# Score products of two attention maps: full-height products first, half-height rests side by side, mask added on VectorE

## The chip, the core and the metric

The kernel runs on one core of a Trainium2 chip. The metric is the device time of one execution in microseconds. The names used below: PE is TensorE's matmul, PEld its weight load, DVE is VectorE, ACT is ScalarE, POOL is GpSimd, SP is the engine that issues most DMAs.

## What is computed

A decoder block on 1024 tokens of width 1024. Two mixers run in parallel, a differential attention of 4 heads and a short gated convolution. They are merged by sigmoid gates, projected and normalised, and a routed mixture of 32 experts (two per token) follows. The change lies in the attention alone, cut here to its core:

```python
s = jnp.einsum('bhmqd,bhmkd->bhmqk', qi, kt) * scale     # m: two maps, head width 64
mask = kpos[None, :] <= qpos[:, None]
p = jax.nn.softmax(jnp.where(mask, s, neg), axis=-1)
a = p[:, :, 0] - lam * p[:, :, 1]
return jnp.einsum('bhqk,bhkv->bhqv', a, vt)              # in blocks of 128 queries
```

## The kernel before, in words

The program runs in stages. First come the projections of q, k and v (`first_part`, products `psq` of 256 columns, lines 372 to 374) and the convolution branch (`pc`). Then comes the attention, from about 306 us to 603 us of the trace. Merging projections (`projections`), the mixing product with routing (`mixing`), and the experts with the last normalisation follow.

The attention loops over 4 heads and, in each, over 8 blocks of 128 queries; block i has (i + 1) * 128 keys (`kw`). Heads 0 to 2 take the blocks in rising order, head 3 in falling order. For each block `scores` makes two score maps, and `values` turns the pair of the block before into the head's output. Between the two stand the gate products (`gates`, tile `psg`, lines 389 to 391): 24 products of 512 columns per call, two calls per block for the first 4 blocks and one for each later block, until after 28 blocks all 32 calls are used up. The last 4 blocks of head 3 (512 keys and fewer) have none.

Every factor of a score is split into a high and a low part, so that q k = qh kh + ql kh + qh kl. The head width is 64, half of TensorE's 128 rows, and `prep` uses that: `kh` holds the high part of k twice, on both halves of the rows, and `qh` holds the high part of q on one half and the low part on the other. So one product over all 128 rows (line 478) gives qh kh + ql kh, the combined product. The rest, qh kl, is a product over 64 rows (line 481): rows 0 to 63 for map 0 and rows 64 to 127 for map 1, since that is where `qh` and `kl` of the map lie. Scores are made in pieces of up to 512 columns, at least 256 wide.

Before the rest of a map's last piece, line 480 multiplies an identity by the mask tile (`identb`, `maskb`, 128 columns, bf16) and accumulates that on the block's diagonal. Then VectorE takes the row maxima (line 483), ScalarE the exponentials with their sums (line 485), and `values` scales them (lines 493 to 496), transposes the result on TensorE (line 503, `tp`), copies it out of PSUM on VectorE (line 504, `ct`) and multiplies by v (line 507, `po`). The score tiles come from the pool `psc` with 2 buffers of 1024 columns.

A scheduler orders the instructions of each engine when the program is built; the chip runs each engine's list in order. The core of a map's products:

```python
T.matmul(ps[:, c:c + n], q, kh[:, c:c + n], start=True, stop=False)
if c + 512 >= kw:
    T.matmul(ps[:, i * P:kw], K.identb, K.maskb, start=False, stop=False, skip_group_check=True)
T.matmul(ps[:, c:c + n], q[a], kl[:, c:c + n], start=False, stop=True)
```

Of the kernel before, what the change touches and what calls it, by code (L numbers as in the profile page):

```python
# [11 lines left out]
F32 = mybir.dt.float32  # L12
F32R = mybir.dt.float32r
BF16 = mybir.dt.bfloat16
# [8 lines left out]
P = 128  # L23
S = 1024
# [151 lines left out]
def constants(K):  # L176
    nc, tc = K.nc, K.tc
    G, V = nc.gpsimd, nc.vector
    const = K.const
    K.ident = const.tile([P, P], F32, name="ident")  # L180
    make_identity(nc, K.ident)

    K.cols = const.tile([P, 48], F32, name="cols")

    K.lam = const.tile([P, 2], F32, name="lam")
    K.epss = const.tile([P, 1], F32, name="epss")
    K.epsc = const.tile([P, 1], F32, name="epsc")
    G.memset(K.epsc, EPS)
    K.one1 = const.tile([P, 1], F32, name="one1")
    K.maskb = const.tile([P, P], BF16, name="maskb")  # L190
    K.identb = const.tile([P, P], BF16, name="identb")
    V.tensor_copy(K.identb, K.ident)
    K.ssq = const.tile([P, HEADS, NT], F32, name="ssq")

    K.L = const.tile([P, NT, 40], F32, name="L")
    K.gm = const.tile([P, NT, 8], F32, name="gm")
    K.em = const.tile([P, NT, 8], F32, name="em")

    K.aw = const.tile([P, NT, 2], F32, name="aw")

    K.second = const.tile([P, N_COLS], F32, name="second")
    K.gidx = const.tile([P, N_COLS], I32, name="gidx")
    K.sidx = const.tile([P, N_COLS], I32, name="sidx")

    K.rows = const.tile([P, 256], F32, name="rows")

    K.order = const.tile([P, 32], I32, name="order")
    K.over = const.tile([P, 32], I32, name="over")
    K.omax = const.tile([P, 1], I32, name="omax")
    dram = K.dram  # L210

    K.h_dram = dram.tile([S, DW], F32, name="h_dram")

    K.y_dram = dram.tile([2 * S, D], F32, name="y_dram")
    K.y_views = dram_disjoint_views(K.y_dram, N_COLS)
    K.g_dram = dram.tile([P, 16, S], F32, name="g_dram")
    K.z_dram = dram.tile([P, 4, 2, S], F32, name="z_dram")
# [71 lines left out]
def first_part(K, stL, stR):  # L289
# [3 lines left out]
    V, A, G, T, SY = nc.vector, nc.scalar, nc.gpsimd, nc.tensor, nc.sync  # L293
# [29 lines left out]
    with ExitStack() as st:  # L323
# [38 lines left out]
        for c in range(6):  # L362
# [3 lines left out]
            for tb in range(NT):  # L366
                if c == 0 and tb >= 2:
                    load_x(tb)
                ps = psb.tile([P, 512], F32, name="psq")[:, 0:256]
# [25 lines left out]
    with ExitStack() as st:  # L395
        cv = st.enter_context(tc.tile_pool(name="cv", bufs=2, side="right", reuse_waits="tile"))
        pc = st.enter_context(tc.tile_pool(name="pc", bufs=5, space=PSUM, reuse_waits="tile"))
        n = 0
# [40 lines left out]
    sc = ExitStack()  # L439
    psc = sc.enter_context(tc.tile_pool(name="psc", bufs=2, space=PSUM, reuse_waits="tile"))  # L440
# [6 lines left out]
    def prep(h):  # L447

        kh = [kq.tile([P, S], F32R, name=f"kh{m}") for m in range(2)]
        kl = kq.tile([P, S], F32R, name="kl")  # L450
        qh = [kq.tile([P, S], F32R, name=f"qh{m}") for m in range(2)]
        for src, is_k in ((ks, True), (qs, False)):
            for g in range(2):
                gs = slice(g * 512, g * 512 + 512)
                ps = ps1.tile([P, 512], F32, name="tp")
                for b in range(4):
                    T.transpose(ps[:, b * P:(b + 1) * P], src[g][:, b, h * P:(h + 1) * P], ident)
                for m, (a, b) in enumerate(((LO, HI), (HI, LO))):
                    if is_k:
                        A.copy(kh[m][a, gs], ps[a])  # L460
                        V.tensor_sub(kl[a, gs], ps[a], kh[m][a, gs].bitcast(F32))
                        G.tensor_copy(kh[m][b, gs], kh[m][a, gs].bitcast(F32))
                    else:
                        A.copy(qh[m][a, gs], ps[a])
                        V.tensor_sub(qh[m][b, gs], ps[a], qh[m][a, gs].bitcast(F32))
        return [(kh[m], kl[a], qh[m], a) for m, a in enumerate((LO, HI))]

    def scores(maps, i):
        kw = (i + 1) * P
        res = []  # L470
        s = sm.tile([P, 2], F32, name="s")
        for m in range(2):
            kh, kl, qh, a = maps[m]
            ps = psc.tile([P, S], F32, name="sc")
            for c in range(0, kw, 512):
                n = max(256, min(512, kw - c))
                q = qh[:, i * P:(i + 1) * P]
                T.matmul(ps[:, c:c + n], q, kh[:, c:c + n], start=True, stop=False)
                if c + 512 >= kw:
                    T.matmul(ps[:, i * P:kw], K.identb, K.maskb, start=False, stop=False, skip_group_check=True)  # L480
                T.matmul(ps[:, c:c + n], q[a], kl[:, c:c + n], start=False, stop=True)  # L481
            nm = sm.tile([P, 1], F32, name="nm")
            V.tensor_reduce(nm, ps[:, 0:kw], axis=AX.X, op=ALU.max, negate=True)  # L483
            p = pp.tile([P, S], F32, name=f"p{m}")
            A.activation(p[:, 0:kw], ps[:, 0:kw], AF.Exp, bias=nm, scale=1.0, accum_out=s[:, m:m + 1])  # L485
            res.append(p)
        return res, s
# [50 lines left out]
    n = 0  # L538
    maps = prep(0)
    for h in range(HEADS):  # L540
        for i in order(h):
            cur = scores(maps, i)
            for _ in range(2 if n < 8 else 1):
                if n < 32:
                    gates(n)
                    n += 1
                    if n == 32:
                        sx.close()
                        open_proj(K, stL, w1, piece)
            if pend is not None:  # L550
                values(*pend)
            pend = (h, i, *cur)
            if i == 3 and h + 1 < HEADS:
                nxt = prep(h + 1)
        if h + 1 < HEADS:
            maps = nxt
# [920 lines left out]
@with_exitstack  # L1477
def block_kernel(ctx: ExitStack, tc: tile.TileContext, x, positions, w_in, b_gate, lq1, lk1, lq2, lk2, subln_g,
                 w_o_att, conv_w, w_o_conv, w_mix, ln1_g, ln1_b, w_rg, b_rg, w_re, b_re, w_eg, w_eu, w_ed,
                 ln2_g, ln2_b, out):  # L1480
    K = Ctx()
    for name, ap in list(locals().items()):
        if name not in ("ctx", "K"):
            setattr(K, name, ap)
    K.nc = tc.nc
    K.const = ctx.enter_context(tc.tile_pool(name="const", bufs=1, side="left"))
    K.dram = ctx.enter_context(tc.tile_pool(name="dram", bufs=1, space=DRAM))
    constants(K)
    K.stM = ctx.enter_context(ExitStack())
    K.stP = ExitStack()  # L1490
    stL, stR = ExitStack(), ExitStack()
    first_part(K, stL, stR)
    projections(K, stR)
    K.stP.close()
    mixing(K, stL, stR)
    stR.close()
    experts(K)
    combine(K)
    K.stM.close()
# [22 lines left out]
```

## Time and profile before

| | |
|---|---|
| device time, median of 3 runs | 1428.47 us (1427.58 to 1430.57) |
| the profiled execution | 1428.7 us, of which the span of its instructions is 1426.7 us |
| PE busy | 1308.1 us, 92% of the span |
| DVE busy | 697.0 us, 49% |
| ACT busy | 487.5 us, 34% |
| DMA | 301.75 MB, mean 211 GB/s |
| mean granted TensorE clock | 0.966 |

The busy time of PE counts each matmul from its start to the end of its results, and matmuls overlap like that: what one costs is read from the distance between the starts of neighbours. In the timeline rows the first number is the start in us and the second the duration; an "xN" at the end merges N equal neighbours.

### The profile page before, as it was taken

To read this page: it belongs to the slowest core of one execution; us is meant where nothing else is said; L and a number is where in the kernel's file an instruction comes from. 1 tells how busy PE (TensorE), PEld (TensorE's weight loads), DVE (VectorE), ACT (ScalarE), POOL (GpSimd) and SP (SyncE) were. 2 spreads that over 40 slices of the span, in tenths; PEclk is the share of its full clock that TensorE was granted. 3 is DMA by queue.
4 is the path that set the end of the run, shared out by engine and by line. 5 is a ranking of instruction groups with operands and counts; after the bars stand their busy time and mean duration, and the time that the engine had idled before them with its cause. 6 is when DMAs were issued, how large, how long until landed. Compare 5 with 4: busy or idle time off the path is not lost. (4 is left out here: it accounts for less than half of the span.)

```text
span 1426.7 us, 17850 instructions
## 1 busy us (share of the span) xinstructions
PE 1308.1 (92%) x6771; PEld 938.4 (66%) x6771; DVE 697.0 (49%) x1254; ACT 487.5 (34%) x837; POOL 137.3 (10%) x213
## 2 busy tenths in 40 slices
PE   7999999999999999999999948999999998999830
PEld 7999888877777777778788735654555544454310
DVE  6431133243535355476566656654554544453338
ACT  4102111144545455442221235532343333342125
POOL 1330000000000001000000120000110011000005
PEclk9999999999999999999999969999999999999975
DMA  7112121122121310364654277699999999999946
GB/s 241 52 39 60 45 74 60 59 74 75 46 73 53 104 59 16 140 224 148 216 206 148 104 227 275 241 414 421 420 420 402 409 419 419 420 409 406 420 182 242
DMA packets 101240, 301.75 MB, mean 211 GB/s; under 512 B 13550, under 2 KB 56603, under 8 KB 76571
## 3 DMA queue, kind: packets, MB, share of 16 engines
q1 hardware_dynamic: 93370, 279.54, 51.4%
q0 software_dynamic: 7776, 21.00, 3.8%
q8 instruction: 55, 0.90, 0.3%
q14 instruction: 39, 0.31, 0.1%
HBM read 274.81 MB, written 33.04 MB: 216 GB/s over the span
## 5 line engine op out<-in xcount | busy, mean ns | idle before, releaser
L173 DVE TENSOR_TENSOR wlo<-m,whi 128x1024 fp32r<-128x1024 f32 x72 | 87.1, 1223 | 70.6 <-ACT whi L172 68.3
L372 PE MATMUL psq<-wh,xh 128*128 128x256 f32 x384 | 109.3, 285 | 0.7 <-ACT xh L172 0.7
L373 PE MATMUL psq<-wl,xh 128*128 128x256 f32 x384 | 108.2, 282 | 0.0
L374 PE MATMUL psq<-wh,xl 128*128 128x256 f32 x384 | 107.7, 281 | 0.0
L172 ACT CAST wh<-wr 128x1024 fp32r<-128x1024 f32 x41 | 43.0, 1052 | 187.3 <-PE pc L390 64.9
L389 PE MATMUL psg<-xh,wh 128*128 128x512 f32 x256 | 104.9, 410 | 0.0
L391 PE MATMUL psg<-xh,wl 128*128 128x512 f32 x256 | 102.2, 399 | 0.0
L390 PE MATMUL psg<-xl,wh 128*128 128x512 f32 x256 | 102.1, 399 | 0.0
L172 ACT CAST whi<-m 128x1024 fp32r<-128x1024 f32 x72 | 74.6, 1050 | 58.1 <-PE g L1075 20.4
L173 DVE TENSOR_TENSOR wl<-wr,wh 128x1024 fp32r<-128x1024 f32 x41 | 51.8, 1266 | 82.8 <-ACT wh L172 82.6
L761 PE MATMUL pm<-wmh,m 128*128 128x512 f32 x256 | 77.1, 406 | 0.0
L390 PE MATMUL pc<-xl,wh 128*128 128x512 f32 x192 | 75.9, 396 | 0.0
L389 PE MATMUL pc<-xh,wh 128*128 128x512 f32 x192 | 75.9, 396 | 0.0
L391 PE MATMUL pc<-xh,wl 128*128 128x512 f32 x192 | 75.9, 395 | 0.0
L372 PEld LDWEIGHTS psq<-wh,xh 128*128 128x128 f32 x384 | 72.9, 190 | 1.5 <-ACT xh L172 1.4
L373 PEld LDWEIGHTS psq<-wl,xh 128*128 128x128 f32 x384 | 73.1, 190 | 0.0
L374 PEld LDWEIGHTS psq<-wh,xl 128*128 128x128 f32 x384 | 72.9, 190 | 0.2 <-DVE xl L173 0.2
L485 ACT ACTIVATE p<-sc,nm 128x128 f32<-128x128 f32 (+7 forms) x64 | 47.4, 741 | 48.3 <-DVE nm L483 20.5
L504 DVE COPY ct<-tp 128x512 f32<-128x512 f32 (+3 forms) x48 | 26.7, 557 | 72.6 <-PE tp L503 72.3
L483 DVE TENSOR_REDUCE nm<-sc 128x1 f32<-128x128 f32 (+7 forms) x64 | 48.4, 756 | 28.2 <-PE sc L481 28.0
L389 PEld LDWEIGHTS psg<-xh,wh 128*128 128x128 f32 x256 | 48.1, 188 | 13.9 <-issue 2.6
L391 PEld LDWEIGHTS psg<-xh,wl 128*128 128x128 f32 x256 | 48.1, 188 | 10.7
(429 smaller groups left out, 2924.5 us busy)
## 6 DMA issues: line engine op xcount, KB each, us to landing
m<-in_w_exp_down_dram SPq DMA_DIRECT2D x32, 1024.0 KB, 20.1
m<-in_w_exp_up_dram SPq DMA_DIRECT2D x32, 1024.0 KB, 20.6
m<-in_w_exp_gate_dram SPq DMA_DIRECT2D x24, 1024.0 KB, 19.8
wr<-in_w_in_dram SPq DMA_DIRECT2D x40, 512.0 KB, 4.3
raw<-in_w_exp_down_dram SPq DMA_DIRECT2D x20, 1024.0 KB, 20.8
raw<-in_w_exp_up_dram SPq DMA_DIRECT2D x13, 1024.0 KB, 13.1
raw<-in_w_exp_gate_dram SPq DMA_DIRECT2D x12, 1024.0 KB, 20.1
rawY<-in_w_exp_gate_dram SPq DMA_DIRECT2D x12, 1024.0 KB, 21.1
```

What stands on the lines that cost most here:

```text
L172: nc.scalar.copy(hi, raw)
L173: nc.vector.tensor_sub(lo, raw, hi.bitcast(F32))
L372: T.matmul(ps, xh[:, k, ts], wh[k], start=k == 0, stop=False)
L373: T.matmul(ps, xh[:, k, ts], wl[k], start=False, stop=False)
L374: T.matmul(ps, xl[:, k, ts], wh[k], start=False, stop=k == KD - 1)
L389: T.matmul(ps, hi[:, k], xh[:, k, hs], start=k == 0, stop=False)
L390: T.matmul(ps, hi[:, k], xl[:, k, hs], start=False, stop=False)
L391: T.matmul(ps, lo[:, k], xh[:, k, hs], start=False, stop=k == KD - 1)
L483: V.tensor_reduce(nm, ps[:, 0:kw], axis=AX.X, op=ALU.max, negate=True)
L485: A.activation(p[:, 0:kw], ps[:, 0:kw], AF.Exp, bias=nm, scale=1.0, accum_out=s[:, m:m + 1])
L504: V.tensor_copy(ct[:, g * P:(g + nb) * P], ps[:, 0:nb * P])
L761: T.matmul(ps[:, hs], a[:, k], w[:, hs], start=k == 0 and i == 0, stop=k == KD - 1 and i == 2)
```

## The change

`scores` now takes both maps' tiles at once. It issues the combined products of map 0 and of map 1 for all pieces, and then the rests piece by piece, map 0 and map 1 in turn, so that a product on the upper half of the rows stands beside one on the lower half. The identity product is gone, and with it `identb` and its cast. In its place VectorE adds `maskb` to the diagonal 128 columns of each score tile in PSUM, ahead of the row maxima. Nothing else is edited.

```diff
--- before.py
+++ after.py
@@ -188,8 +188,6 @@
     G.memset(K.epsc, EPS)
     K.one1 = const.tile([P, 1], F32, name="one1")
     K.maskb = const.tile([P, P], BF16, name="maskb")
-    K.identb = const.tile([P, P], BF16, name="identb")
-    V.tensor_copy(K.identb, K.ident)
     K.ssq = const.tile([P, HEADS, NT], F32, name="ssq")
 
     K.L = const.tile([P, NT, 40], F32, name="L")
@@ -469,16 +467,18 @@
         kw = (i + 1) * P
         res = []
         s = sm.tile([P, 2], F32, name="s")
+        pss = [psc.tile([P, S], F32, name="sc") for _ in range(2)]
+        parts = [(c, max(256, min(512, kw - c))) for c in range(0, kw, 512)]
+        for ps, (kh, kl, qh, a) in zip(pss, maps):
+            for c, n in parts:
+                T.matmul(ps[:, c:c + n], qh[:, i * P:(i + 1) * P], kh[:, c:c + n], start=True, stop=False)
+
+        for c, n in parts:
+            for ps, (kh, kl, qh, a) in zip(pss, maps):
+                T.matmul(ps[:, c:c + n], qh[a, i * P:(i + 1) * P], kl[:, c:c + n], start=False, stop=True)
         for m in range(2):
-            kh, kl, qh, a = maps[m]
-            ps = psc.tile([P, S], F32, name="sc")
-            for c in range(0, kw, 512):
-                n = max(256, min(512, kw - c))
-                q = qh[:, i * P:(i + 1) * P]
-                T.matmul(ps[:, c:c + n], q, kh[:, c:c + n], start=True, stop=False)
-                if c + 512 >= kw:
-                    T.matmul(ps[:, i * P:kw], K.identb, K.maskb, start=False, stop=False, skip_group_check=True)
-                T.matmul(ps[:, c:c + n], q[a], kl[:, c:c + n], start=False, stop=True)
+            ps = pss[m]
+            V.tensor_add(ps[:, i * P:kw], ps[:, i * P:kw], K.maskb)
             nm = sm.tile([P, 1], F32, name="nm")
             V.tensor_reduce(nm, ps[:, 0:kw], axis=AX.X, op=ALU.max, negate=True)
             p = pp.tile([P, S], F32, name=f"p{m}")
```

The built program has 96 products with `kh` and 96 with `kl`, as before, and 64 identity products fewer on TensorE; VectorE has 64 additions more and the cast of `identb` less. The lists of POOL and SP are the same as before, and from the merging projections' middle on those of the other engines too. Lines shift by 2 or more: 474 is the combined product, 478 the rest, 481 the addition.

**TensorE, head 3, block 4 (640 keys, pieces of 512 and 256).** Before (`kh_4264` and `qh_4267` are map 0's, `kh_4265` and `qh_4268` map 1's):

```order
L478 MATMUL sc<-kh_4264,qh_4267 128x512
L481 MATMUL sc<-kl,qh_4267 128x512
L478 MATMUL sc<-kh_4264,qh_4267 128x256
L480 LDWEIGHTS identb
L480 MATMUL sc<-maskb,identb 128x128
L481 MATMUL sc<-kl,qh_4267 128x256
L478 MATMUL sc<-kh_4265,qh_4268 128x512
L507 MATMUL po<-vs,ct 128x128 x4
L503 MATMUL tp<-ident,p_4709 128x128 x3
L481 MATMUL sc<-kl,qh_4268 128x512
L478 MATMUL sc<-kh_4265,qh_4268 128x256
```

After (map 0: `qh_4265`, map 1: `qh_4266`):

```order
L474 MATMUL sc<-kh_4262,qh_4265 128x512
L474 MATMUL sc<-kh_4262,qh_4265 128x256
L474 MATMUL sc<-kh_4263,qh_4266 128x512
L474 MATMUL sc<-kh_4263,qh_4266 128x256
L478 MATMUL sc<-kl,qh_4265 128x512
L507 MATMUL po<-vs,ct 128x128 x4
L503 MATMUL tp<-ident,p_4712 128x128 x3
L478 MATMUL sc<-kl,qh_4266 128x512
L478 MATMUL sc<-kl,qh_4265 128x256
L478 MATMUL sc<-kl,qh_4266 128x256
```

The four combined products now stand together. The first rest of map 0 is followed by products over all rows (`po`, `tp`) of the block before; behind them three rests stand in a row, on halves in turn.

**TensorE, head 3, block 3 (512 keys), the first block without gate products.** Before:

```order
L478 MATMUL sc<-kh_4264,qh_4267 128x512
L480 LDWEIGHTS identb
L480 MATMUL sc<-maskb,identb 128x128
L481 MATMUL sc<-kl,qh_4267 128x512
L478 MATMUL sc<-kh_4265,qh_4268 128x512
L480 LDWEIGHTS identb
L480 MATMUL sc<-maskb,identb 128x128
L481 MATMUL sc<-kl,qh_4268 128x512
L507 MATMUL po<-vs,ct 128x128 x4
```

After:

```order
L474 MATMUL sc<-kh_4262,qh_4265 128x512
L474 MATMUL sc<-kh_4263,qh_4266 128x512
L478 MATMUL sc<-kl,qh_4265 128x512
L478 MATMUL sc<-kl,qh_4266 128x512
L507 MATMUL po<-vs,ct 128x128 x4
```

Two visits to the half-height products have become one, and both identity products are gone.

**VectorE, head 1, around block 4's copies out of PSUM (`ct`, 512 and 128 columns).** Before:

```order
L504 COPY ct<-tp 128x512
L483 TENSOR_REDUCE nm<-sc 128x1
L493 RECIPROCAL r<-s 128x2
L173 TENSOR_TENSOR wl<-wr,wh 128x1024
L504 COPY ct<-tp 128x512
L483 TENSOR_REDUCE nm<-sc 128x1
L494 TENSOR_TENSOR r<-r,lam 128x2
L504 COPY ct<-tp 128x128
```

After:

```order
L481 TENSOR_TENSOR sc<-sc,maskb 128x128
L493 RECIPROCAL r<-s 128x2
L483 TENSOR_REDUCE nm<-sc 128x1
L504 COPY ct<-tp 128x512
L481 TENSOR_TENSOR sc<-sc,maskb 128x128
L494 TENSOR_TENSOR r<-r,lam 128x2
L483 TENSOR_REDUCE nm<-sc 128x1
L504 COPY ct<-tp 128x128
```

The 512-column copy, on which the next `po` of TensorE waits, stood behind a row maximum, and now stands behind an addition of the mask and a row maximum; another addition has come between it and the 128-column copy.

Over the whole program, counted in these lists: a rest stands behind a product over all rows in 96 places before and in 55 places after (and as often the other way round). After, 35 of the 96 rests stand straight behind a rest on the other half of the rows (21 times the one ahead is 512 columns wide, once 384, 13 times 256), and 6 behind one on the same half.

## Rows read from the trace of the kernel before

**Rows 1.** The page: busy time of TensorE and VectorE.

```profile
PE 1308.1 (92%) x6771; PEld 938.4 (66%) x6771; DVE 697.0 (49%) x1254; ACT 487.5 (34%) x837; POOL 137.3 (10%) x213
```

**Rows 2.** Busy time by stretch; PE, PEld, DVE, ACT, POOL, then granted clock, DMA share, GB/s.

```profile
300.00:580.00 280.00, 280.00 (x1347) 212.51 (x1345) 133.73 (x220) 133.28 (x288) 17.13 (x20) 1.00 0.18 60
580.00:610.00 30.00, 29.48 (x166) 22.83 (x165) 15.34 (x37) 15.31 (x50) 0.00 (x0) 1.00 0.48 174
...
940.00:1360.00 420.00, 399.13 (x1960) 206.89 (x1960) 192.66 (x223) 144.71 (x182) 37.29 (x33) 0.99 1.01 415
```

**Rows 3.** Timeline, PE, gate products: start us, duration us, engine, line, operation.

```profile
440.68 0.40 PE L389 MATMUL psg<-xh,wh 128*128 128x512 f32 x1
440.91 0.40 PE L390 MATMUL psg<-xl,wh 128*128 128x512 f32 x1
```

**Rows 4.** Timeline, PE, products of 256 columns in the first stage.

```profile
100.23 0.28 PE L372 MATMUL psq<-wh,xh 128*128 128x256 f32 x1
100.35 0.28 PE L373 MATMUL psq<-wl,xh 128*128 128x256 f32 x1
```

**Rows 5.** Timeline, PE, head 3, query block 4 (640 keys).

```profile
578.49 0.48 PE L478 MATMUL sc<-kh,qh 128*128 128x512 f32 x1
578.89 0.49 PE L481 MATMUL sc<-kl,qh 64*128 64x512 f32 x1
579.32 0.38 PE L478 MATMUL sc<-kh,qh 128*128 128x256 f32 x1
579.54 0.23 PE L480 MATMUL sc<-maskb,identb 128*128 128x128 bf16 x1
579.70 0.38 PE L481 MATMUL sc<-kl,qh 64*128 64x256 f32 x1
580.01 0.50 PE L478 MATMUL sc<-kh,qh 128*128 128x512 f32 x1
580.35 1.05 PE L507 MATMUL po<-vs,ct 128*128 128x128 f32 x8
581.24 0.49 PE L503 MATMUL tp<-ident,p 128*128 128x128 f32 x3
```

**Rows 6.** Timeline, PE, head 3, query block 3 (512 keys).

```profile
589.51 0.47 PE L478 MATMUL sc<-kh,qh 128*128 128x512 f32 x1
589.83 0.23 PE L480 MATMUL sc<-maskb,identb 128*128 128x128 bf16 x1
589.98 0.50 PE L481 MATMUL sc<-kl,qh 64*128 64x512 f32 x1
```

**Rows 7.** Groups by line and form, 300 to 606 us: busy us, mean ns, idle before.

```profile
L480 PE MATMUL sc<-maskb,identb 128*128 128x128 bf16 x64 | 14.6, 228 | 0.0
...
L483 DVE TENSOR_REDUCE nm<-sc 128x1 f32<-128x128 f32 x8 | 2.3, 287 | 3.1 <-PE sc L481 3.1
L504 DVE COPY ct<-tp 128x128 f32<-128x128 f32 x7 | 2.0, 292 | 15.1 <-PE tp L503 15.1
```

**Rows 8.** Waits, 300 to 612 us: who for whom, us in total, times, longest.

```profile
DVE ct L504 <- PE tp L503: 72.3, 40, 8.0
...
DVE nm L483 <- PE sc L481: 28.0, 40, 2.0
...
PEld po L507 <- DVE ct L504: 1.3, 3, 0.8
...
PE po L507 <- DVE ct L504: 0.5, 1, 0.5
```

**Rows 9.** The page: the score reduction over all its forms.

```profile
L483 DVE TENSOR_REDUCE nm<-sc 128x1 f32<-128x128 f32 (+7 forms) x64 | 48.4, 756 | 28.2 <-PE sc L481 28.0
```

**Rows 10.** Waits of SP's queue, 600 to 940 us.

```profile
SPq L1047 <- PE g L1238: 38.1, 3, 21.4
...
SPq L1047 <- PE pm L761: 16.4, 7, 3.3
```

## The prediction

> **What bounds the kernel now.** I read the views from coarse to fine. The page says that TensorE is busy for 92% of the span and VectorE for 49% [rows 1]; that is a mean over stages, so the stage that the change touches comes next. In the table by stretch, TensorE has no idle time at all between 300 and 580 us, the granted clock is 1.00 (the 2.4 GHz level), VectorE is busy for 133.7 of the 280 us and the DMA engines for 18% [rows 2]. The attention is bound by TensorE's list of instructions, so the question is how much time its list takes, and a matmul's price there is the distance from its start to the next start, not its duration.
>
> The timeline gives these distances. A regular product of 512 columns (each with a weight load of its own) takes 440.91 - 440.68 = 0.23 us [rows 3], one of 256 columns 0.12 us [rows 4]. The scores don't keep that pace. In block 4 of head 3 [rows 5] the full-height 512-column product is followed by its half-height rest after 578.89 - 578.49 = 0.40 us, and the rest by the next full-height product after 0.43 us. So going to half height costs 0.40 - 0.23 = 0.17 us beyond the columns, and coming back 0.43 - 0.23 = 0.20 us. After the 256-column rest it is 580.01 - 579.70 = 0.31, less 0.12, so 0.19 us: the cost doesn't hang on the width. One visit to half height costs about 0.37 us. The identity product stands between: 0.22 us from the 256-column product to it and 0.16 us from it to the rest [rows 5], together 0.38 us, where 0.12 + 0.17 = 0.29 us would do without it. At 512 columns it is 589.98 - 589.51 = 0.47 us [rows 6] against 0.40 us. So an identity product costs 0.07 to 0.09 us of TensorE's time, not the 228 ns of its row [rows 7].
>
> **The change, part by part.**
>
> *Visits to half height.* The order of the change has 55 of them where there were 96, so 41 fewer: 41 x 0.37 = 15.2 us less. It is not 32 (one for each block), since the scheduler puts `po` and `tp` between the rests in many blocks, as in block 4 shown above.
>
> *Identity products.* 64 are gone at 0.08 us, the middle of the two prices: 5.1 us less.
>
> *Rests side by side.* 35 rests stand straight behind a rest on the other half of the rows. The trace of before holds no such pair, so their distance has to be bounded. If the second simply runs behind the first at the regular pace it is 0.23 us at 512 columns and 0.12 at 256: no further gain. If the two overlap fully it is near 0, which saves 21 x 0.23 + 1 x 0.18 + 13 x 0.12 = 6.6 us (0.18 for 384 columns is halfway between the two prices). If changing halves stalls as changing heights does, it is 0.43 and 0.31 us, which costs 35 x 0.20 = 7.0 us. I take an overlap at the pace of weight loads, since each rest brings its own: eight `po` products of 128 columns with a load each take 581.24 - 580.35 = 0.89 us, 0.11 us apiece [rows 5], the tightest pace at which such loads follow each other there. The saving is then 21 x 0.12 + 0.07 + 13 x 0.01 = 2.7 us.
>
> The Trainium skill (TensorE: Matmul & The Clock Gate, Part 3) has matmuls on different row groups start about 4 ns apart; by it this term would be the full 6.6 us. No row here shows such a pair.
>
> *The addition on VectorE.* 64 instructions on 128 columns out of PSUM. Two rows of that size are near: the row maximum takes 287 ns and the copy `ct` 292 ns [rows 7]; I take 0.29 us, 18.6 us in all. In the stretch to 580 us TensorE's full list covers it: VectorE would be busy for some 150 of about 260 us, and it is VectorE that waits for TensorE (72.3 us for `tp`, 28.0 us for scores), while TensorE waited 1.3 + 0.5 = 1.8 us for VectorE's copies [rows 8]. Each addition does lengthen the way from score to exponential by 0.29 us, but that result is wanted only in the next block, behind 24 gate products of 0.23 us, 5.6 us. The cover ends with the gate products: the last 4 blocks of head 3 have none, and there 8 additions stand on a chain that TensorE may wait for. If all of that shows it is 8 x 0.29 = 2.3 us, if none does 0. The convolution's first products fill in there and TensorE is busy for 29.5 of the 30 us up to 610 us [rows 2], so I take half, 1.2 us more.
>
> *Taking both score tiles at once.* Map 1's first product now starts before map 0's rest, so the exponentials of the block before must have read both tiles somewhat earlier. With 5.6 us of gate products between, I cost this at nothing; in the last 4 blocks it is part of the 1.2 us.
>
> *The cast of `identb`* is gone from VectorE's start: 0.2 us at most, left out.
>
> *Behind the attention.* SP's list is unchanged. From 940 to 1360 us the DMA engines are saturated (share 1.01, 415 GB/s) [rows 2], so a gain lasts only if those loads start earlier too. They do: before 940 us the queue with the expert weights waits on TensorE's products (38.1 us and 16.4 us in two rows) [rows 10], which free its buffers, and these come earlier by what the attention gains. So I pass the gain on whole.
>
> **Sum**: -15.2 - 5.1 - 2.7 + 1.2 = -21.8 us. The sum is made against the profiled execution, 1428.7 us, which is 0.2 us above the median of the three runs: 1428.7 - 21.8 = 1406.9 us, or 1.5% less.
>
> **The rivals.**
>
> *A. The halves overlap fully.* 6.6 us in place of 2.7, and no loss in the last blocks: -15.2 - 5.1 - 6.6 = -26.9, 1401.8 us. For it: the two rests use different rows of the array and write different score tiles. Against it: each rest's weight load is an instruction of its own, and none in the rows follows another at less than 0.11 us.
>
> *B. Changing halves stalls like changing heights.* +7.0 in place of -2.7: -15.2 - 5.1 + 7.0 + 1.2 = -12.1, 1416.6 us. For it: both other changes of the array's use stall in rows 5. Against it: there the height changes; here it stays.
>
> *C. VectorE takes TensorE's place.* In the order shown, a `ct` copy stands behind an addition and a row maximum, and both wait for TensorE's rests; `po` waits for that copy, and everything behind `po` on TensorE with it. If TensorE has to wait out one such pair in each of the 32 blocks, 0.29 us plus the 0.756 us of a mean row maximum [rows 9], that is 1.05 x 32 = 33.6 us against the gain of 15.2 + 5.1 + 2.7 = 23.0: 1428.7 + 10.6 = 1439.3 us, slower. It decides the sign where the wait passes 23.0 / 32 = 0.72 us a block. Against it stand VectorE's half-idle time [rows 2] and the 1.8 us of such waits now [rows 8]; for it, that the order was made with estimated times. The Trainium skill (TensorEngine Tiling (Array Packing), PSUM Bottleneck) warns of just this: packing speeds up the matmuls but not what empties PSUM, which may become the limit. The 72.3 us that VectorE waits for `tp` speak against that here.
>
> *D. The gain is partly handed back behind the attention*, because a load or another wait in the merging and mixing stages ends where it did. If half is lost: 1428.7 - 10.9 = 1417.8 us. Against it: the waits of rows 10.
>
> **How the numbers follow.** My forecast has a chance of 0.60; it runs from 1404 us (no loss in the last blocks) to 1410 us (no overlap at all, -15.2 - 5.1 + 1.2 = -19.1, so 1409.6). A gets 0.13, B 0.13, C 0.08, D 0.06. The range that leaves out 2 in 10 goes from just below A, 1401 us, to B and D, 1417.5 us; C lies outside, with parts of B and D. Within 0.2% (2.9 us, about what a measurement of this kernel can tell from no change) the cases leave little: 0.03, from a mild C. Slower by more has 0.05, the rest of C. Faster has 0.92.
>
> **What would show it.** In the changed profile, the stretch from the first score product to the last should be some 22 us shorter, with the gate products at their 0.23 us. In the timeline a rest behind a rest on the other half should start about 0.11 us after it (A: near 0; my upper bound 0.23; B: 0.43 at 512 columns). Leaving half height should still cost about 0.20 us and entering it 0.17 us. The additions should take about 0.29 us each, and TensorE's waits for `ct` stay below 4 us in all; under C they would be 20 us and more. The saturated DMA stretch should begin and end some 22 us earlier; under D it would not. I am wrong if the attention shrinks by less than 15 us, or if the stages behind it grow by more than 3 us.

## The result and the profile after

The changed kernel takes 1409.28 us (median of 4 runs, 1407.85 to 1410.37). The kernel before, run beside it, takes 1428.24 us (1427.58 to 1430.57). The ratio is 0.9864, with a 95% interval of 0.9847 to 0.9881: 19.0 us or 1.4% faster. The forecast was 1406.9 us. It missed by 2.4 us, inside its range.

The profiled execution took 1409.53 us, its span 1407.6 us, 19.2 us less than before. The page of the changed kernel and its busy time by stretch (columns as in [rows 1] and [rows 2]):

```profile
PE 1285.1 (91%) x6707; PEld 924.4 (66%) x6707; DVE 710.4 (50%) x1317; ACT 487.2 (35%) x837; POOL 135.9 (10%) x213
```

```profile
300.00:560.00 260.00, 259.83 (x1295) 201.19 (x1293) 144.74 (x274) 133.44 (x288) 15.57 (x20) 1.00 0.20 64
560.00:590.00 30.00, 27.74 (x157) 21.30 (x156) 17.32 (x49) 15.28 (x50) 0.00 (x0) 1.00 0.53 179
...
920.00:1340.00 420.00, 399.22 (x1958) 207.00 (x1958) 193.01 (x223) 144.60 (x181) 37.56 (x33) 0.99 1.01 415
```

Against [rows 1], TensorE lost 23.0 us of busy time and VectorE gained 13.4. TensorE's list stays full in the attention, at a granted clock of 1.00, so its length was still what bounded the stage. The last 30 us are less full than in [rows 2], 27.74 us busy where 29.48 were; most of the missing time are two waits that are read below. In windows of 20 us, the saturated DMA stretch of 420 us has moved 20 us forward and is no shorter.

**The stretch that shrank.** I measure it from the first score product to the first transposes of the merging stage (line 664), the same work in both kernels but for the identity products. Here are its ends on TensorE in the timeline, before:

```profile
306.01 0.36 PE L478 MATMUL sc<-kh,qh 128*128 128x256 f32 x1
...
606.88 0.47 PE L507 MATMUL po<-vs,ct 128*128 128x128 f32 x2
607.11 0.70 PE L588 MATMUL psg<-zh,wl 128*128 128x512 f32 x2
...
609.05 0.60 PE L664 MATMUL tp<-ident,qs 128*128 128x128 f32 x4
...
611.36 0.63 PE L664 MATMUL tp<-ident,qs 128*128 128x128 f32 x4 [1.28 <-DVE ol L666]
```

And after:

```profile
306.68 0.36 PE L474 MATMUL sc<-kh,qh 128*128 128x256 f32 x1
...
561.87 0.61 PE L478 MATMUL sc<-kl,qh 64*128 64x512 f32 x3
562.21 0.28 PE L478 MATMUL sc<-kl,qh 64*128 64x256 f32 x1
562.41 0.50 PE L387 MATMUL psg<-xh,wh 128*128 128x512 f32 x1
562.75 0.39 PE L388 MATMUL psg<-xl,wh 128*128 128x512 f32 x1
...
569.46 0.40 PE L474 MATMUL sc<-kh,qh 128*128 128x512 f32 x1
569.79 0.49 PE L478 MATMUL sc<-kl,qh 64*128 64x512 f32 x2
570.21 1.16 PE L507 MATMUL po<-vs,ct 128*128 128x128 f32 x8
...
586.97 0.47 PE L507 MATMUL po<-vs,ct 128*128 128x128 f32 x2
587.20 0.71 PE L588 MATMUL psg<-zh,wl 128*128 128x512 f32 x2
587.75 0.60 PE L664 MATMUL tp<-ident,qs 128*128 128x128 f32 x4
...
591.40 0.63 PE L664 MATMUL tp<-ident,qs 128*128 128x128 f32 x4 [2.61 <-DVE ol L666]
```

(The row at 562.21 is the third of the three rests merged in the row at 561.87. It and the row at 569.46, the combined product of map 1, come from narrower windows, which don't merge them.)

Before, the stretch is 609.05 - 306.01 = 303.04 us. After, it is 587.75 - 306.68 = 281.07 us: 22.0 us less. The forecast's sum was 21.8. From the first score product to the last, which starts at 602.78 before and at 582.14 after, it is 21.3 us less; to the last two `po` products (606.88 and 586.97) it is 20.6.

The most telling row is the one at 569.79. It merges two rests of 512 columns with a duration of 0.49 us, which is the duration of one [rows 5]: they run at the same time, one on each half of the array. In the trace the second starts 4 ns behind the first, and the next product follows at 570.21, 0.42 us behind both. Before, one rest alone took 0.43 us to the next start [rows 5]. In the row at 561.87 the first two of three rests overlap likewise, and the third starts 0.34 us behind them.

**VectorE's side**, groups by form and waits, 300 to 590 us and 300 to 920 us of the changed kernel:

```profile
L481 DVE TENSOR_TENSOR sc<-sc,maskb 128x128 f32<-128x128 f32 x64 | 17.6, 293 | 12.2 <-PE sc L478 11.2 <-ACT gt L534 0.9
```

```profile
DVE ct L504 <- PE tp L503: 59.1, 30, 7.4
...
PE ptp L1200 <- DMA xs<-h_dram,gidx: 10.3, 1, 10.3
...
PEld po L507 <- DVE ct L504: 3.2, 9, 0.6
...
PE tp L664 <- DVE ol L666: 2.6, 1, 2.6
...
PE sc L474 <- ACT p L485: 0.9, 1, 0.9
```

An addition takes 293 ns (forecast 0.29 us). TensorE's weight loads wait 3.2 us for `ct` (1.3 in [rows 8]), under the 4 us that I had named. VectorE still waits for TensorE far more than the other way. One wait is new against [rows 8]: a score product stands 0.9 us for the exponential of an earlier block (`sc` for `p`). Two have grown: the transposes of line 664 for `ol`, from 1.28 us in the row of before above to 2.61, and `ptp` for a gather, from 8.9 us in the same view of the kernel before:

```profile
PE ptp L1200 <- DMA xs<-h_dram,gidx: 8.9, 1, 8.9
```

### The profile page after: what moved, and what is told of

It is laid out like the page before. It is cut to its first block, busy times and chain, and to the rows that moved or that the text cites. A ratio compares the mean times of both kernels' runs of the same rounds, so it can differ in the third digit from the quotient of the medians.

```text
span 1407.6 us, 17784 instructions
## 1 busy us (share of the span) xinstructions
PE 1285.1 (91%) x6707; PEld 924.4 (66%) x6707; DVE 710.4 (50%) x1317; ACT 487.2 (35%) x837; POOL 135.9 (10%) x213
## 5 line engine op out<-in xcount | busy, mean ns | idle before, releaser
L388 PEld LDWEIGHTS psg<-xl,wh 128*128 128x128 f32 x256 | 48.1, 188 | 11.1 <-issue 0.9
L173 DVE TENSOR_TENSOR wlo<-raw,whi 128x1024 fp32r<-128x1024 f32 x30 | 36.2, 1223 | 37.4 <-ACT whi L172 36.3
```

The lines of the kernel that those rows point to most:

```text
L173: nc.vector.tensor_sub(lo, raw, hi.bitcast(F32))
L388: T.matmul(ps, hi[:, k], xl[:, k, hs], start=False, stop=False)
```

## The experiments

The table puts them side by side. "Stretch" runs from the first score product to the first transposes of line 664, each read off that kernel's profiled execution. Visits and overlapped pairs (rests that start at most 14 ns behind another) are counted there too. The kernel before had a median of 1429.81 us in the runs beside the first four experiments, and 1428.62 beside the last four, so the ratios compare better than the medians do. In "early table load" and "full height, early table load" the scheduler put two `po` products behind the end of the stretch.

| kernel | visits | overlapped | stretch, us | median, us | ratio to before (95%) |
|---|---|---|---|---|---|
| before | 96 | 0 | 303.04 | 1428.24 | |
| mask on VectorE alone | 96 | 0 | 299.81 | 1429.09 | 0.9996 (0.9986 to 1.0005) |
| order alone, identity product kept | 47 | 33 | 282.33 | 1412.50 | 0.9875 (0.9858 to 0.9893) |
| all rests on the same half | 55 | 0 | 284.84 | 1414.91 | 0.9892 (0.9874 to 0.9909) |
| the change | 55 | 23 | 281.07 | 1409.28 | 0.9864 (0.9847 to 0.9881) |
| rests over the full height | 0 | 0 | 267.88 | 1401.91 | 0.9798 (0.9783 to 0.9814) |
| one visit a block | 32 | 48 | 270.31 | 1401.69 | 0.9812 (0.9800 to 0.9825) |
| early table load | 55 | 23 | 280.66 | 1411.33 | 0.9879 (0.9865 to 0.9893) |
| full height, early table load | 0 | 0 | 267.86 | 1397.89 | 0.9788 (0.9775 to 0.9801) |
| the same with the identity product | 0 | 0 | 274.01 | 1402.29 | 0.9821 (0.9808 to 0.9833) |

### The mask alone

The order of before, without the identity product and with the addition on VectorE:

```diff
-                if c + 512 >= kw:
-                    T.matmul(ps[:, i * P:kw], K.identb, K.maskb, start=False, stop=False, skip_group_check=True)
...
+            V.tensor_add(ps[:, i * P:kw], ps[:, i * P:kw], K.maskb)
```

> The products in the order of before (96 visits to half height), but the mask added by VectorE as in the change. By the forecast the 64 identity products are worth 5.1 us less the 1.2 us that the additions cost in the last blocks: 3.9 us faster than before, about 1424.5 us. Rival that fits the trace of the change: in the trace of before, 34 of the identity products stand as the second product after a visit to half height and only inherit the 0.10 us that any such product shows; then an identity product itself is worth 0.07 us or less, and the gain is 2 to 4.5 us. Rival C (VectorE's additions stall TensorE): not faster, 1428 us or more.

The stretch shrank by 3.2 us (3.9 expected), and the time did not change. That is the time of rival C, but not its mechanism, since TensorE's stretch did get shorter. The gain is gone again before the end: three waits and stalls of its trace say where. The waits:

```profile
PE ptp L1197 <- DMA xs<-h_dram,gidx: 10.3, 1, 10.3
...
PE tp L661 <- DVE ol L663: 2.6, 1, 2.6
```

and busy time by stretch, behind the transposes:

```profile
605.00:610.00 5.00, 2.39 (x17) 2.02 (x18) 3.67 (x7) 4.40 (x9) 0.00 (x0) 0.98 0.90 276
610.00:615.00 5.00, 5.00 (x20) 4.02 (x20) 4.17 (x6) 3.94 (x6) 0.00 (x0) 0.68 0.46 147
```

TensorE reached the transposes 3.2 us earlier, and waited there 1.3 us longer (2.6 against 1.3). It was busy for only 2.39 of those 5 us; in the next 5 us the granted clock was 0.68, part of it at the lower level of 1.2 GHz, where the kernel before had no such dip. The products `pa` behind it took 81.25 us from first to last, against 79.68 before. The gather's wait was longer by 1.4 us. That is 1.3 + 1.6 + 1.4 = 4.3 us in this one execution, more than the gain; no run shows each of the three by itself.

### The order alone

The change with the identity product put back behind each map's combined products, in place of the addition.

```diff
+            T.matmul(ps[:, i * P:kw], K.identb, K.maskb, start=False, stop=False, skip_group_check=True)
...
-            V.tensor_add(ps[:, i * P:kw], ps[:, i * P:kw], K.maskb)
```

> The order of the change (combined products of both maps first, rests on halves in turn), but the mask is the identity product on TensorE as before; its order has 47 visits in place of 96. By the forecast's prices: 49 x 0.37 = 18.1 us for visits, and 49 pairs instead of 35, about 4 us: 22 us faster than before, 1406 us, so about 3 us faster than the change. If the pairs overlap fully and a visit costs 0.41 us as counted in both traces, 20 to 24 us faster than before. If the additions on VectorE are what made the change fast, it would be 15 us or less.

Nearly the whole gain comes from the order: 1412.5 us, and 20.7 of the 22.0 us of the stretch. I had expected it 3 us under the change; it lies 3 us above it, and the two intervals overlap. It isn't a pure test of the mask, as the scheduler made another order of it, with 47 visits and 33 overlapped pairs.

### The halves not in turn

The change's own order, with both maps' rests on rows 0 to 63, so that nothing can overlap:

```diff
-        return [(kh[m], kl[a], qh[m], a) for m, a in enumerate((LO, HI))]
+        return [(kh[m], kl[LO], qh[m], LO) for m in range(2)]
```

> The change, instruction for instruction in the same order on every engine, but map 1's rest is made on rows 0 to 63 as well, from map 0's low part of k and the high half of the other q tile: map 1's scores are not what the reference computes. No two rests can then run at once. The trace of the change shows 23 of its pairs starting 4 ns apart; rests on the same half start 0.33 us apart. If the halves are what lets them overlap, these 23 pairs cost about 0.2 to 0.33 us each: 5 to 7 us slower than the change, about 1415 us. If any two half-height rests in a row would do as well, it is as fast as the change.

The stretch is 3.8 us longer than the change's, and the time about 4 us by the ratios, whose intervals overlap. The rests of block 3 of head 3 in the timeline, 512 columns each, as in the changed kernel's row at 569.79:

```profile
571.82 0.73 PE L478 MATMUL sc<-kl,qh 64*128 64x512 f32 x2
572.48 1.16 PE L507 MATMUL po<-vs,ct 128*128 128x128 f32 x8
```

Two rests now take 0.73 us together where they took 0.49, and the next product starts 572.48 - 571.82 = 0.66 us behind the first, against 0.42. So the overlap is worth 0.24 us for a pair at 512 columns, the whole price of the second rest.

This kernel has the change's visits without its overlap, so against the kernel with the mask alone it prices the visits by themselves: 299.81 - 284.84 = 15.0 us for 41 fewer, 0.365 us each.

### No visits at all

If the price is that of changing height, rests over all 128 rows should cost no more columns and no visits. POOL copies `kl` to the other half too, and the rest multiplies `qh` whole, which adds the small product ql kl to the scores.

```diff
+                        G.tensor_copy(kl[m][b, gs], kl[m][a, gs].bitcast(F32))
...
-        return [(kh[m], kl[a], qh[m], a) for m, a in enumerate((LO, HI))]
+        return [(kh[m], kl[m], qh[m], slice(0, P)) for m in range(2)]
```

> The order of the change, but no half-height product at all: the low part of k stands on both halves of the rows in a tile for each map (POOL copies it, as it copies the high part), and the rest is a product over all 128 rows with the same stationary tile as the combined product (it adds the product of the two low parts, which before was left out). If the visits are what a score costs beyond its columns, all that the trace of the change shows for them goes: entering 7.0, leaving 8.7, the product after leaving 5.6, the slower product ahead of entering 2.7, waiting for a busy half 2.4, less the 4.3 us that overlap gave: 22 us faster than the change, about 1387 us. If the half-height products run at once and pay for their visits, it is no faster than the change. Rival: POOL's 28 more copies of 0.66 us delay the first scores of a head: then 15 us.

It is faster than the change: 1401.91 us, 7 us less in the medians and 9 by the ratios. I had expected 22. The same block in its timeline:

```profile
556.53 0.62 PE L479 MATMUL sc<-kl,qh 128*128 128x512 f32 x2
557.01 1.16 PE L508 MATMUL po<-vs,ct 128*128 128x128 f32 x8
```

Two rests take 557.01 - 556.53 = 0.48 us, twice the regular 0.23 and no stall, which is 0.06 us more than the overlapped pair with its exit. In the trace the combined product ahead takes 0.23 us as well. The stretch lost 13.2 us. The 55 visits at 0.365 us are 20.1 us, less the 3.8 us of the lost overlap, so 16.3 were due. (The expectation's items come to 26.4 us for these visits, too much by 6. It also counted 28 more copies on POOL. The trace has 16, and no wait of TensorE for them.) Of the missing 3.1 us, 2.8 lie in distances from a gate product or a `po` to the next `po`, which are longer than in the change. The weight loads of `po` wait longer for VectorE's copy `ct` here, 5.3 us in 19 places, where the change has 3.2 us in 9:

```profile
PEld po L508 <- DVE ct L505: 5.3, 19, 0.6
```

That these waits are the cause was not tested. Then 8.4 of the 35.2 us that the stretch has gained on before are handed back by the span's end (26.8 us less), 3.8 of them between the first transposes and the first `pa`, though 16 products stand there in place of 12.

### One visit in each block

The change with the rests held together by order dependences and a higher priority in the scheduler, so that each of the 32 blocks has one visit.

```diff
+            hp.enter_context(tc.high_priority())
             for c, n in parts:
                 for ps, (kh, kl, qh, a) in zip(pss, maps):
-                    T.matmul(...)
+                    mm = T.matmul(...)
+                    tc.add_manual_dep(mm.ins, last.ins.name, ...)
```

> The change with the rests held together: dependencies of order only keep the rests of a block in turn behind its last combined product, at high priority, so that no product of another kind comes between. The order then has 32 visits in place of 55, one a block, and 64 rests behind one on the other half in place of 35. The runs so far give 0.37 us for a visit (15.0 us of the score stretch for 41 visits, the same-half kernel against the mask-alone kernel), so 23 x 0.37 = 8.4 us, and some 9 more pairs that overlap, about 1.5 us: the stretch from the first to the last score some 8 to 10 us shorter than with the change. Theory that the stages behind hand back what the last blocks' chain can't follow: 1 to 2 us of it is lost at the transposes behind the attention, so 6 to 9 us faster than the change, 1400 to 1403 us. Rival: the copies that TensorE's other products wait for come later relative to it, and the time goes into new waits: no faster than the change.

1401.69 us, some 7.5 us under the change, as expected. Four rests of 512 columns stand together in its timeline:

```profile
518.06 0.73 PE L480 MATMUL sc<-kl,qh 64*128 64x512 f32 x4
518.73 1.16 PE L511 MATMUL po<-vs,ct 128*128 128x128 f32 x8
```

They take 0.67 us, what two take one after the other on the same half. The stretch is 10.8 us shorter than the change's. The 23 visits less are worth 8.4 us, and the 25 more overlapped pairs, at the prices given below, some 5 us where I had expected 1.5; what became of the rest I did not trace. The forecast was right that the change would not come down to 32 visits, and these are the microseconds that it left.

### The end of the attention

The changed kernel's last steps on ScalarE, in the timeline:

```profile
587.48 0.27 ACT L508 COPY qs<-po 128x128 f32<-128x128 f32 x1 [0.58 <-PE po L507]
587.65 0.28 ACT L510 ACTIVATE junk<-po 128x128 f32<-128x128 f32 x1
587.81 0.20 ACT L510 ACTIVATION_READ_ACCUMULATOR junk<-po 128x1 f32 x1
588.04 1.28 ACT L517 ACT_TABLE_LOAD   x1
589.33 0.30 ACT L517 ACTIVATE ssq<-ssq,epss 128x8 f32<-128x8 f32 x1
589.54 0.67 ACT L665 ACTIVATE oh<-tp,cols 128x512 fp32r<-128x512 f32 x1
```

The copy of the last block's output, the sum of its squares, a table load of 1.28 us and the root stand ahead of the `oh` copies of the transposes, which `ol` waits for. TensorE has its transposes started at 587.75, and ScalarE comes to them at 589.54. Before, it came at 609.75, 0.70 us behind the transposes' start; now 1.79 us behind. A tiny square root ahead of the last block's output was to bring the table load forward:

```diff
+        if last:
+            tc.keep_in_program_order(A.activation(K.one1, K.epsc, AF.Sqrt))
```

> The change, with one tiny ScalarE activation of the square root kind put behind the last block's scaling, so that ScalarE's load of the table for the last head's scale (1.28 us, which in the trace of the change stands between the last copy of the head's output and the copies oh that TensorE's transposes wait for) is done while ScalarE waits. If that chain is what handed back 1.3 us at the transposes (a wait of 2.6 us in place of 1.3), the wait falls to about 1.3 us or less and the kernel is 1 to 1.5 us faster than the change, and TensorE's clock is less often granted at half behind the wait: up to 3 us in all. If the wait is set by something else (the additions of the mask in the last block, a DMA), no difference.

It gained nothing: 1411.33 us, with a ratio of 0.9879 (0.9865 to 0.9893) where the change has 0.9864 (0.9847 to 0.9881). The table load did move (to 583.74). But the scheduler also put the first transposes ahead of the last two `po` products, and 22 products in place of 12 stand from there to the first `pa`. The wait of 2.6 us fell apart into several:

```profile
PE tp L666 <- DVE ol L668: 0.7, 1, 0.7
PE tp L666 <- DVE ssq L520: 0.7, 1, 0.7
PE po L666 <- ACT junk L512: 0.6, 1, 0.6
PE pa L590 <- ACT woh L172: 0.4, 1, 0.4
```

Behind them the granted clock fell (columns as in [rows 2]), which it did not in the profile of the change:

```profile
590.00:595.00 5.00, 3.99 (x16) 3.05 (x17) 4.67 (x7) 3.86 (x7) 0.00 (x0) 0.66 0.63 214
```

So the table load is one link of a chain, of which the sum of squares, the reciprocal and the scaling are others. What the load costs by itself this kernel does not show, since order and clock changed with it.

The same edit was also put into the full-height version, so that the two diffs stand in one kernel:

> The full-height rests with the early table load. The full-height kernel lost 3.8 us at the transposes and 1.8 us more behind them, where TensorE's clock was granted at 0.50 for a stretch of 6.8 us, against the trace of before. If both come from the 2.8 us wait at the transposes, the early load gives 1.3 us of the wait back and the clock stays up: 2 to 5 us faster than the full-height kernel, 1397 to 1400 us. If the clock falls all the same, 1 us.

This is the full-height version with the early table load, the fastest version here: 1397.89 us, some 11 us under the change. Its ratio, 0.9788 (0.9775 to 0.9801), and that of the full-height version alone, 0.9798 (0.9783 to 0.9814), overlap, so the table load's part in it is not shown.

And that kernel with the identity product in place of the addition, as in the diff of the order alone:

> As the last, with the mask as the identity product on TensorE instead of VectorE's addition. Without visits to half height there is no stall that the identity product could fill, so it costs TensorE its own pace, some 0.07 us and whatever its change of type costs: 64 x 0.07 to 0.17 = 4.5 to 11 us of the score stretch; it takes 2 x 0.29 us off the last block's chain. So 3 to 10 us slower than the last. If the mask's place doesn't matter at all, as in the mask-alone kernel, the same.

It is 4.4 us slower in the medians and 6.2 us longer in the stretch. Up to the last `po`, which stands behind the first transposes in the one kernel and ahead of them in the other, it is 5.2 us longer. That is 0.08 to 0.10 us for each of the 64 products. Where no change of height stalls TensorE, the identity product costs its whole price, and the addition's 0.9 us of waiting is the better bargain.

## Why the prediction was right, and where it was off

The three terms of the stretch came to 15.0, 3.2 and 3.8 us where the forecast had 15.2, 3.9 and 2.7. That their sum agrees to 0.2 us is luck in part: the errors, -0.2, -0.7 and +1.1 us, nearly cancel. The lower end of the forecast's inner range was worked out wrongly, too: without a loss in the last blocks its terms give 1428.7 - 23.0 = 1405.7 us, not 1404.

**Visits to half height: right, 15.0 us measured for 15.2.** The price of 0.37 us held, but the runs show its parts more finely. In the changed kernel's rows the third rest at 562.21 is followed by a gate product after 0.20 us, where 256 columns take 0.12: leaving costs 0.08. That product is followed after 562.75 - 562.41 = 0.34 us, so 0.11 more. Likewise the third rest came 0.34 us behind the first pair, 0.11 over the regular 0.23. And entering behind the full-height product at 569.46 took 0.33 us, 0.10 over it. So a change of height costs 0.08 to 0.10 us, and the first product behind it holds TensorE 0.10 to 0.11 us longer than its columns: its row lasts 0.50 us at 562.41, the next one's 0.39. The weight loads show what goes with that:

```profile
562.41 0.19 PEld L387 LDWEIGHTS psg<-xh,wh 128*128 128x128 f32 x1 [0.25 <-issue]
562.52 0.19 PEld L388 LDWEIGHTS psg<-xl,wh 128*128 128x128 f32 x1
```

The load of the first product behind the change starts with its product. The load of the next one runs under the product ahead, from 562.52 for a product at 562.75. It is so at all 192 changes of height before and all 110 after, where the load starts 1 or 2 ns ahead of its product; of the stretch's other products the median is 229 ns. A visit has both charges twice, 0.38 us. Where a product stands alone between two changes, its own charge and that of the next change fall into one distance, nearly so in the 0.17 and 0.20 us of [rows 5].

The Trainium skill (TensorEngine Tiling (Array Packing), Key Properties) says that a change of tiling mode drains TensorE, a change of tile doesn't. The rows agree in their times: a change of height costs, a change to the other half, where that is idle, takes 4 ns at most. That a drain is what takes the time they do not show.

**Rests side by side: rival A's mechanism, 3.8 us for 2.7.** The step that failed is "I take an overlap at the pace of weight loads". The weight loads don't hold a rest back when it goes to an idle half: 23 rests of the changed kernel start 1 to 4 ns behind the one on the other half. But A's 6.6 us did not come either, since both A and I counted all 35 rests that stand behind one on the other half. In 12 of these places the half that the rest goes to is still at work, as at 562.21, where the third rest goes to the half that the first one holds. These save nothing. Both counts also priced a pair by its first rest, and where 256 columns stand beside 512 only the shorter one is saved. Against the same pairs on one half, the 23 pairs save what their second rest costs: 0.23 us in nine pairs of 512 columns, 0.115 in eight of 256, 0.12 in five of 512 and 256, and 0.17 in one of 384. That is 3.8 us, and so is the difference of the two stretches.

The Trainium skill (TensorE: Matmul & The Clock Gate, Part 3, The mechanism) has matmuls on different row groups start about 4 ns apart, and the trace agrees. The same place says that a weight load overlaps a running matmul only where the row groups differ. Here the measurement differs and decides. With all rests on one half, the load of the second of the two at 571.82 starts at 571.93, under the first one on the same rows and 0.23 us ahead of its own product. Products of one height do the same in general, with the 229 ns above.

**Identity products and additions: right in sum, 3.2 us for 5.1 - 1.2 = 3.9.** Against the distances in the kernel with the mask alone, an identity product cost the kernel before 0.07 us in the 34 places where its combined product stands behind a rest, 0.09 in 16 others, and 0.05 in 12 where a `po` or `tp` stands ahead of it: some 4.5 us for all. Every kernel with the addition has the wait of 0.9 us of a score product for an exponential, and the three with the identity product (before, the order alone, the full height with it) have none. That is the price of the additions that I had put at half of 2.3 us, and it stands in the last 4 blocks, where I looked for it.

**"So I pass the gain on whole": this step failed, by 2.8 us.** The stretch gave 22.0 us, and the span 19.2. Of the difference, 0.7 us lies ahead of the stretch (its first product starts at 306.68 in place of 306.01, in a part that was not edited; in the ten profiles it starts at 304.58 to 306.68), 1.3 us in the longer wait of the transposes and 1.4 us in the longer wait for the gather; the rest is -0.6. These are two executions. The interval of the ratio allows a gain of 17.0 to 21.9 us, so that something was lost is only just clear of it.

The first of these waits is real for this change: the mask alone has it as well, and the order alone has 2.1 us. From the last two `po` products to the third group of transposes it is 611.36 - 606.88 = 4.48 us before and 591.40 - 586.97 = 4.43 us after. TensorE's list got shorter, this way through ScalarE and VectorE did not. What stood in it is what changed: eight of the convolution's products (`psg` from `zh` and `zl`) before, two in the change. The other six stand earlier in its list. The gather's wait was 8.8 to 10.3 us in the ten profiles, and 8.9 and 8.8 in kernels whose gains differ by 30 us. I take it for a matter of the execution, not of the change, but no run was made on it alone. The loads behind did move as argued: the saturated stretch begins 20 us earlier. Rival D named the place rightly and the size wrongly (half of the gain).

**The other rivals.** B (a stall at each change of halves) is excluded by the 4 ns, C (VectorE binds) by TensorE's 259.83 of 260 us and the 3.2 us of waits for `ct`. From the first transposes to the end it takes 2.2 us more than before, under the 3 us that I had named as a sign of being wrong.

## What to carry to other kernels

Price each change between full-height and half-height products as a stall of its own, read from distances between starts, and count the visits in the instruction order, not in the source. Before packing halves side by side, ask whether the same factor can be put on both halves: here full-height rests, with no visit at all, beat the packed ones by 7 us or more, and kept pace with packed ones that had one visit a block. A gain on the bounding engine is whole only up to the point where that engine waits for the others' last steps; with the gain of 3 us from the mask alone, nothing of it reached the end.

## What the hardware showed that was not expected

- Two 64-row products on different halves start 1 to 4 ns apart, each with a weight load of about 183 ns of its own.
- The first product behind a change of height lasts 0.10 us longer, and its weight load starts with it, not under the product ahead. The identity product's load, bf16 behind fp32r products, starts with it as well in 52 of its 64 places in the kernel before, as for the one at 579.54 in [rows 5].
- TensorE's clock can fall where a faster stage leaves TensorE with pauses. In seven of the ten profiles a stretch at 0.50 lies right behind the transposes; in those of the kernel before, the change and the last of the table it does not. In the full-height kernel with the early table load, TensorE was busy for 2.66 and 2.00 of two stretches of 4 us, with no pause longer than 0.74 us, and then ran at a granted clock of 0.50, the 1.2 GHz level:

```profile
572.00:576.00 4.00, 2.66 (x17) 1.76 (x15) 1.43 (x4) 2.86 (x12) 0.00 (x0) 1.00 0.55 171
576.00:580.00 4.00, 2.00 (x11) 1.41 (x11) 3.98 (x7) 2.90 (x4) 0.00 (x0) 0.74 1.02 338
580.00:584.00 4.00, 4.00 (x14) 3.31 (x14) 3.51 (x7) 2.29 (x4) 0.00 (x0) 0.50 0.95 340
```

The changed kernel has one pause of 2.61 us there, and kept its clock in the profiled execution:

```profile
584.00:588.00 4.00, 3.82 (x22) 2.66 (x21) 1.71 (x7) 2.23 (x12) 0.00 (x0) 1.00 0.11 34
588.00:592.00 4.00, 1.39 (x13) 1.16 (x12) 3.31 (x7) 3.78 (x7) 0.00 (x0) 1.00 1.02 308
```

The mask alone has a pause of the same 2.61 us, and its clock fell. Whether the change keeps it in every execution stays open, as does what the longer waits for `ct` cost the full-height kernels.
